# Query and key weights loaded by whole pages, their 32-column runs picked by the readers, and rows sorted by head at the store

## The chip, the cores and the metric

The kernel runs on one core of a Trainium2 chip. A core has a matrix engine (TensorE, PE in the profile, with its weight loads listed as PEld), a vector engine (VectorE, DVE), an engine for functions of one element (ScalarE, ACT), a general one (GpSimd, POOL) and a queue engine that mainly issues transfers (SyncE, SP). Each engine takes its instructions in a fixed order, and an instruction that waits holds all that stand behind it. Transfers run on 16 DMA engines; SP's are issued one after another, in the order in which the program was written. Matrix products are accumulated in PSUM banks, from which ACT or DVE moves them on.

The metric is the device time of one execution, in microseconds (us), as the median of several runs.

## The reference

The kernel computes one layer of an encoder block over 1024 tokens of width 1024, in float32. One input projection feeds two branches. Branch A is a windowed attention with three groups of eight heads of 64 dimensions, whose windows step by 1, 4 and 16 tokens. Branch B is a gated recurrence. Both are gated, projected, merged and added to the input.

What the change touches is the making of queries and keys in branch A:

```python
h = rms_norm(h_res, norm_w[layer])
z = jnp.einsum('bsd,dc->bsc', h, w_in[layer])
...
q = rms_norm(qkv_a[:, :, g, 0], q_norm_w[layer, g])   # over the 64 dimensions of a head
k = rms_norm(qkv_a[:, :, g, 1], k_norm_w[layer, g])
o_g, m_g, d_g = dilated_window_attention(q, k, v, bias, window, dilation)
```

## The kernel before, in words

**Stages.** The kernel goes through the input norm and the value projections (to about 141 us of the span), a stage of block products (to about 686), attention mixed with other products (to about 860), the recurrence (to about 1250) and the output projections.

**Block products.** A block is a product of 1024 x 256 weights with all tokens. Its weights are cut into quarters: two halves of the contraction (first digit) by two column halves of 128 (second digit), "11", "12", "21", "22", each a page of 128 partitions x 512 floats. Seven products are made instead of eight, of sums and differences of quarters: "11", "T1", "T2", "21", "T3", "22", "T4" (`run_quads`). Each of the seven is 12 matmuls in three passes per four pieces, because a float32 weight is split into a high part `whi` and a low part `wlo`. ACT makes `whi`; POOL makes `wlo`, or DVE for "T2" and "T4" (`LOWS`, line 33); DVE forms the differences in place in the raw page (line 445). There are 27 blocks: 12 of queries or keys ("qk", by group, half of the heads, and query or key), and 15 of other columns.

**Pages and rings.** Raw quarters lie in a ring `qraw` of `QRAW` = 6 buffers of 128 x 512 (line 1112); split pages lie in rings `whi` and `wlo` of `RING` = 9 buffers, which all stages share (lines 25, 349). A page is split only when its number is below the count of freed pages plus `RING` (lines 369, 437). The normalisation of queries and keys has a ring `ny` of four buffers (line 1117); the other rings are `spare` and `stage`.

**The columns of a qk block.** A page of the stored weights holds 256 query columns and then 256 key columns, four heads of 64 each. `block_pages` (line 680) takes for column half 0 the first 32 dimensions of each of the four heads and for half 1 the last 32. So a quarter is four transfers of 64 KB, one per head, in runs of 32 floats (line 413). Thus the two halves of a head lie in the same rows of two tiles, and the sum of squares over a head is one product with a 0/1 matrix (`head_sums`). The chain of each half of the tokens is: squares on ACT, their sum on DVE, split, `head_sums` on PE, logarithm and exponential on ACT (`guess`), a Newton step on DVE, the scaled result on DVE (`scaled`, line 1208), and the store to the scratch tensor `qkD` by SP. For the second and third group, `scaled` also sorts the tokens by their residue mod 4 or 16, and the store writes runs of 128 or 32 floats.

**Attention.** `load_heads` (line 1300) loads queries and keys of four heads as four transfers of 32 partitions each, which puts the dimensions of a head back together; `load_k` and `load_q` call it. The scores of the third group are 64 x 64 products with 64 neighbouring keys of a residue (line 1396).

**Order.** The program orders its own work: a planner (`Plan`) keeps an expected time per engine, with 0.08 us of SP's time for a transfer's issue (line 170), and knows which part of a buffer is written or read when (`_boxes`, which takes a view apart into pieces if its outer dimension is at most 8). A task is emitted when the planner expects its inputs and its buffer soon (`tick`; `Ring.soon`). The order on each engine is fixed by that.

Of the kernel before, what the change touches and what calls it, by code (L numbers as in the profile page):

```python
# [23 lines left out]
WARM = 10  # L24
RING = 9
RAWS = 4
# [3 lines left out]
QB = 6  # L30
QRAW, SPARE = 6, 7
RES = (1, 4, 16)
# [36 lines left out]
def _boxes(ap):  # L69

    if ap.space != SB or ap.ap[0][0] <= 0:
        return ALL
    step, n = ap.ap[0]
    p, lo = divmod(ap.offset, step)
    dims = list(ap.ap[1:])
    starts = [lo]
    while len(dims) > 1 and dims[0][1] <= 8:
        st, m = dims[0]
        if abs(st) <= sum(abs(x) * (k - 1) for x, k in dims[1:]):
            break  # L80
# [147 lines left out]
class Builder:  # L228
# [147 lines left out]
    def split(self, raw, low=None, page=None):  # L376
        hi, lo = self.hir.get(), self.lor.get()
        if self.low == "dma" and page is not None:
            self.p.act.activation(hi, raw, AF.Copy)
            self.p.act.activation(lo, hi.bitcast(F32), AF.Copy, scale=-1.0)  # L380
            self.task("pool", [lo], lambda: self.p.pool.dma_start(lo, page, accum_op=OP.add), 1)
        else:
            self.p.act.activation(hi, raw, AF.Copy)
            getattr(self.p, low or self.low).tensor_tensor(lo, raw, hi.bitcast(F32), op=OP.subtract)
        self.w[self.split_next] = (hi, lo)
        self.split_next += 1
# [18 lines left out]
    def start_quads(self, ring):  # L405

        raw = {}

        def load(m, b):
            raw[m, b] = ring.get()  # L410
            src = self.quads[m][("11", "21", "12", "22").index(b)]
            if isinstance(src, list):
                for i, x in enumerate(src):
                    self.p.sp.dma_start(raw[m, b].rearrange("p (d a c) -> p a d c", d=4, a=4)[:, i], x)
                return
            dst = raw[m, b] if len(src.shape) == 2 else raw[m, b].rearrange("p (d c) -> p d c", d=src.shape[1])
            self.p.sp.dma_start(dst, src)

        for m in range(len(self.quads)):
            for b in ("11", "12", "22", "21"):  # L420
                self.task("sp", [], lambda m=m, b=b: load(m, b), 2, ring.soon)
        work = []
# [10 lines left out]
        at = [0]  # L433
# [7 lines left out]
        def go(k):  # L441
# [6 lines left out]
            for x in {"T3": ("12",), "T4": ("11", "21"), "22": ("22",)}.get(dst, ()):  # L448
                ring.done(raw.pop((m, x)))

# [178 lines left out]
def hybrid_block(ctx, tc, a, out):  # L629
# [50 lines left out]
    def block_pages(kind, *at):  # L680
# [6 lines left out]
        if kind == "gb":  # L687
# [3 lines left out]
        p = 24 * g + 8 + 8 * hv  # L691
        return tuple([_dram(wi, (p + 4 * k) * 65536 + 256 * e + 32 * col + 64 * i, [[512, 128], [65536, 4], [1, 32]])
                      for i in range(4)]
                     for col in range(2) for k in range(2))

# [318 lines left out]
    b.low = "dma"  # L1014
    b.split_next_page()
    at = {0: {11: lambda: root(1)}, 3: {5: lambda: root_out(1), 11: lambda: root(0)}, 7: {5: lambda: root_out(0)}}
    for d in range(8):
        u_products(1, d, at.get(d, {}))
        b.free_to(d + 1)
        if d < 8 - EA:  # L1020
            square(0, EA + d, xs[0, EA + d])()
        if d < 4:
            split_u(1, 4 + d)
        if d < 7:
            b.split_next_page()
        if 3 < d < 7:
            prep_h(1, d - 4, rs["B", 1])
        b.tick()
# [74 lines left out]
    def blocks_start():  # L1103
# [7 lines left out]
        p.tile([128, 16], F32, name="blkPad")  # L1111
        blk["raw"] = b.ring(p, "qraw", QRAW, [128, 512])
        blk["spare"] = b.ring(p, "spare", SPARE, [128, 512])
# [94 lines left out]
    def scaled(g, hv, e, half, z, y2, o, col, count):  # L1208
# [10 lines left out]
        def out():  # L1219
            s_.dma_start(qkD[g, hv, 2 * e + col].rearrange("p (r u) -> p r u", r=R)[:, :, n * half:n * half + n],  # L1220
                         o.rearrange("p (r u) -> p r u", r=R))
            blk["y"].done(o)
# [76 lines left out]

    def load_heads(t, g, hv, k):  # L1300
        for j in range(2):
            for c in range(2):
                s_.dma_start(t[64 * j + 32 * c:64 * j + 32 * c + 32],
                             qkD[g, hv, k + c].rearrange("(a i d) t -> i d a t", a=2, i=2)[j])

    def load_k(g, hv):
        KT[g, hv] = att["k"].get()
        load_heads(KT[g, hv], g, hv, 2)
        score_tasks(g, hv)

    def load_q(g, hv):
        QT[g, hv] = att["q"].get()
        load_heads(QT[g, hv], g, hv, 0)
        score_tasks(g, hv)
# [60 lines left out]
    def scores(g, hv, i0):  # L1375
# [16 lines left out]
        for u in range(2):  # L1392
            k0, n = geo[u][:2]
            for p, e, j in ((p, e, j) for p in range(2) for e in range(2) for j in range(2) if g == 2):
                at = slice(k0 + 64 * e, k0 + 64 * e + 64)
                t_.matmul(pss[u][j][64 * e:64 * e + 64, p, :], q[64 * j:64 * j + 64, p, at], kT[64 * j:64 * j + 64, p, at],
                          start=True, stop=True)
# [1140 lines left out]
```

## Time and profile before

| what | value |
|---|---|
| median of three runs | 1457.58 us (1456.97 to 1460.9) |
| the profiled execution | 1453.19 us |
| its span, from first to last instruction | 1451.4 us |
| PE busy | 1426.0 us, 98% of the span |
| DVE, ACT, POOL busy | 918.3, 859.0, 330.8 us |
| DMA packets | 301347, of which 174963 under 512 B |
| granted PE clock, mean | 0.995 |

The page of the profile gives shares over the whole span. The stretches of the span (busy time of each engine between two points of time, with the count of its instructions), the chain of waits (the work that ended last, followed back) and the timeline of an engine show where time is lost. In the rows, L59 is a helper through which all instructions are issued, so rows are told apart by the names of their tiles: `qA`, `qE`, `qC` are the banks of the block products, `gp` those of the other products, `sc` the scores, `nss` the sums over a head.

### The profile page before, as it was taken

Reading aid. Unit: us, or ns where it says so; the run is one execution under the profiler, and the core shown is the slowest. Engines: PE = TensorE matmul, PEld = TensorE weight load, DVE = VectorE, ACT = ScalarE, POOL = GpSimd, SP = SyncE. Lnnn points to the kernel's source line nnn. Section 1 sums busy time; section 2 is a strip of 40 time slices with the busy share of each in tenths; the row PEclk is TensorE's granted clock in tenths of the full one; section 3 lists DMA queues with packets and bytes.
Section 4 is the critical chain, followed back from the end, with each engine's and each line's share of the span. In section 5 each row is a group of like instructions: output and inputs, shape, how many; then the busy total and the mean of one; then the engine's idle time right before and its main releaser. Section 6 shows DMA issues by size and latency. Waiting matters only on the chain.

```text
span 1451.4 us, 23558 instructions
## 1 busy us (share of the span) xinstructions
PE 1426.0 (98%) x8106; PEld 1182.5 (81%) x8106; DVE 918.3 (63%) x1859; ACT 859.0 (59%) x1852; POOL 330.8 (23%) x356
## 2 busy tenths in 40 slices
PE   9999999998999989999899999999999999999998
PEld 8788787887888868888678878888888888888887
DVE  6673466575666665631355646787878787358973
ACT  7743565554554655644478852397777774548461
POOL 0102335463333323334021000022222221001011
PEclk9999999999999999999999999999999999999999
DMA  7747678987454534533999529864444453678665
GB/s 238 181 143 173 181 205 191 183 179 142 114 117 116 104 74 114 146 102 116 236 255 244 137 76 223 231 169 107 127 108 127 107 135 91 197 257 215 185 171 137
DMA packets 301347, 230.54 MB, mean 159 GB/s; under 512 B 174963, under 2 KB 225419, under 8 KB 300716
## 3 DMA queue, kind: packets, MB, share of 16 engines
q1 hardware_dynamic: 286540, 203.69, 50.4%
q0 software_dynamic: 13824, 25.17, 11.2%
q8 instruction: 64, 1.05, 0.3%
q14 instruction: 55, 0.45, 0.1%
q10 hardware_dynamic: 864, 0.19, 0.1%
HBM read 169.04 MB, written 81.43 MB: 173 GB/s over the span
## 4 chain that ended last, share of the span: by engine, by line
PE 83%; DVE 6%; DMA 4%; ACT 4%; SPq 2%; issue 1%; POOL 0%; DVEq 0%; ACTq 0%
PE gp L59 24%; PE qA L59 19%; PE qE L59 9%; PE sA L59 6%; PE qC L59 5%; PE sE L59 5%; PE u L59 3%; PE oB L59 3%; PE o L59 2%; PE pT L59 2%; PE sc L59 2%; SPq L59 2%; DVE Bc L59 1%; PE U L59 1%; DVE S L59 1%
## 5 line engine op out<-in xcount | busy, mean ns | idle before, releaser
L59 POOL TENSOR_TENSOR wlo<-qraw,whi 128x512 fp32r<-128x512 f32 x135 | 182.3, 1352 | 396.4 <-ACT whi L59 378.5
L59 ACT ACTIVATE whi<-qraw 128x512 fp32r<-128x512 f32 x189 | 118.1, 627 | 116.7 <-PE qA L59 32.6
L59 DVE TENSOR_TENSOR qraw<-qraw,qraw 128x512 f32<-128x512 f32 x108 | 94.1, 872 | 39.4 <-DMA qraw<-in_w_in_dram 32.3
L59 PE MATMUL gp<-hh,whi 128*128 128x512 f32 x264 | 109.7, 415 | 0.0
L59 PE MATMUL gp<-hh,wlo 128*128 128x512 f32 x264 | 103.6, 393 | 0.0
L59 PE MATMUL gp<-hl,whi 128*128 128x512 f32 x264 | 103.0, 390 | 0.0
L59 ACT ACTIVATE as<-as,neg 128x192 f32<-128x192 f32 (+2 forms) x192 | 80.3, 424 | 21.6 <-DVE neg L59 21.5
L59 ACT ACTIVATE whi<-raw 128x512 fp32r<-128x512 f32 x92 | 57.2, 627 | 47.1 <-DMA raw<-in_w_in_dram 21.0
L59 PE MATMUL qA<-hh,whi 128*128 128x512 f32 x216 | 84.0, 389 | 0.0
L59 PE MATMUL qA<-hl,whi 128*128 128x512 f32 x216 | 84.0, 389 | 0.0
L59 PE MATMUL qA<-hh,wlo 128*128 128x512 f32 x216 | 84.0, 389 | 0.0
L59 PE MATMUL gp<-whi,hh 128*128 128x512 f32 x192 | 78.8, 411 | 0.0
L59 POOL COPY mm<-Bc 128x8 f32<-128x8 f32 x64 | 32.6, 539 | 197.7 <-DVE Bc L59 123.3
L59 PE MATMUL gp<-wlo,hh 128*128 128x512 f32 x192 | 75.4, 393 | 0.4 <-DVE wlo L59 0.4
L59 PE MATMUL gp<-whi,hl 128*128 128x512 f32 x192 | 75.2, 392 | 0.0
L59 DVE CUSTOM_DVE_ANT_0 as<-sc,abias 128x192 f32<-128x192 f32 (+2 forms) x192 | 52.0, 326 | 36.3 <-PE sc L59 27.5
L59 DVE TENSOR_TENSOR wlo<-qraw,whi 128x512 fp32r<-128x512 f32 x54 | 37.4, 692 | 56.8 <-ACT whi L59 56.7
L59 DVE TENSOR_TENSOR ny<-ny,spare 128x512 f32<-128x512 f32 x48 | 65.9, 1392 | 0.4
L59 ACT ACTIVATE spare<-qA 128x512 f32<-128x512 f32 x51 | 30.2, 592 | 58.7 <-PE qA L59 57.7
L59 PEld LDWEIGHTS gp<-hh,wlo 128*128 128x128 f32 x264 | 49.5, 188 | 11.0
L59 POOL DMA_DIRECT2D wlo<-in_w_in_dram x36 | 31.3, 870 | 113.8 <-ACT wlo L59 98.0
L59 PEld LDWEIGHTS gp<-hh,whi 128*128 128x128 f32 x264 | 49.8, 189 | 8.3
(309 smaller groups left out, 4118.3 us busy)
## 6 DMA issues: line engine op xcount, KB each, us to landing
raw<-in_w_in_dram SPq DMA_DIRECT2D x84, 256.0 KB, 3.7
qraw<-in_w_in_dram SPq DMA_DIRECT2D x60, 256.0 KB, 3.4
qraw<-in_w_in_dram SPq DMA_DIRECT2D x192, 64.0 KB, 2.7
qkD<-ny SPq DMA_DIRECT2D x48, 256.0 KB, 3.4
wlo<-in_w_in_dram POOLq DMA_DIRECT2D x36, 256.0 KB, 4.3
sg<-sgD SPq DMA_DIRECT2D x32, 256.0 KB, 3.6
eraw<-wsD SPq DMA_DIRECT2D x32, 256.0 KB, 3.4
sgD<-stage SPq DMA_DIRECT2D x26, 256.0 KB, 2.1
```

Of the source, the lines that this page charges most:

```text
L59: got = f(*args, **kw)
```

## The change

Loads: the two column halves of a half of the contraction share one buffer of 128 x 1024 (four such buffers instead of six of 128 x 512). For a qk block one transfer of 512 KB loads both, in runs of 256 floats, and the two quarters are views of it with 16 runs of 32 floats. Other blocks load each quarter into its half of the buffer, as before. A buffer is free when both quarters are done with. Stores: each normalised tile is written by four transfers of 32 rows, to where the head's dimensions lie together in `qkD`. For the keys of the third group, a store no longer puts the two halves of the tokens between each other; the scores pick the keys in two runs of 32. Attention loads queries and keys with one transfer of 1 MB each. The `whi` and `wlo` rings have 8 buffers instead of 9, so one page fewer is split ahead, and in the first stage a split that stood before a loop now is the last of it. `_boxes` takes apart views with up to 16 pieces.

```diff
-RING = 9
+RING = 8
...
-QRAW, SPARE = 6, 7
+QRAW, SPARE = 4, 7
...
-    while len(dims) > 1 and dims[0][1] <= 8:
+    while len(dims) > 1 and dims[0][1] <= 16:
...
     def split(self, raw, low=None, page=None):
-        hi, lo = self.hir.get(), self.lor.get()
+        tiles = hi, lo = self.hir.get(), self.lor.get()
+        if len(raw.shape) == 3:
+            hi, lo = (t.rearrange("p (x i) -> p x i", i=raw.shape[2]) for t in tiles)
...
-        raw = {}
+        raw, pair, left = {}, {}, {}
 
         def load(m, b):
-            raw[m, b] = ring.get()
-            src = self.quads[m][("11", "21", "12", "22").index(b)]
-            if isinstance(src, list):
-                for i, x in enumerate(src):
-                    self.p.sp.dma_start(raw[m, b].rearrange("p (d a c) -> p a d c", d=4, a=4)[:, i], x)
+            half, col = int(b[0]) - 1, int(b[1]) - 1
+            if (m, half) not in pair:
+                pair[m, half] = ring.get()
+                left[m, half] = 2
+            t = pair[m, half]
+            pages = self.quads[m]
+            if len(pages) == 2:
+                for c in range(2):
+                    raw[m, f"{half + 1}{c + 1}"] = t.rearrange("p (x c i) -> p c x i", c=2, i=32)[:, c]
+                self.p.sp.dma_start(t.rearrange("p (d c) -> p d c", d=4), pages[half])
                 return
+            raw[m, b] = t[:, 512 * col:512 * col + 512]
+            src = pages[("11", "21", "12", "22").index(b)]
...
+        def drop(m, b):
+            half = int(b[0]) - 1
+            raw.pop((m, b))
+            left[m, half] -= 1
+            if left[m, half] == 0:
+                ring.done(pair[m, half])
+
         for m in range(len(self.quads)):
-            for b in ("11", "12", "22", "21"):
-                self.task("sp", [], lambda m=m, b=b: load(m, b), 2, ring.soon)
+            for b in ("11", "22") if len(self.quads[m]) == 2 else ("11", "12", "22", "21"):
+                self.task("sp", [], lambda m=m, b=b: load(m, b), 2,
+                          lambda m=m, b=b: (m, int(b[0]) - 1) in pair or ring.soon())
...
-        return tuple([_dram(wi, (p + 4 * k) * 65536 + 256 * e + 32 * col + 64 * i, [[512, 128], [65536, 4], [1, 32]])
-                      for i in range(4)]
-                     for col in range(2) for k in range(2))
+        return tuple(_dram(wi, (p + 4 * k) * 65536 + 256 * e, [[512, 128], [65536, 4], [1, 256]]) for k in range(2))
...
     b.low = "dma"
-    b.split_next_page()
...
-        if d < 7:
-            b.split_next_page()
+        b.split_next_page()
...
-        blk["raw"] = b.ring(p, "qraw", QRAW, [128, 512])
+        blk["raw"] = b.ring(p, "qraw", QRAW, [128, 1024])
...
         def out():
-            s_.dma_start(qkD[g, hv, 2 * e + col].rearrange("p (r u) -> p r u", r=R)[:, :, n * half:n * half + n],
-                         o.rearrange("p (r u) -> p r u", r=R))
+            for i in range(4):
+                to = qkD[g, hv].rearrange("a p t -> (a p) t")[256 * e + 64 * i + 32 * col:256 * e + 64 * i + 32 * col + 32]
+                x = o[32 * i:32 * i + 32]
+                if g == 2 and e == 1:
+                    s_.dma_start(to[:, 512 * half:512 * half + 512], x)
+                else:
+                    s_.dma_start(to.rearrange("p (r u) -> p r u", r=R)[:, :, n * half:n * half + n],
+                                 x.rearrange("p (r u) -> p r u", r=R))
             blk["y"].done(o)
...
-    def load_heads(t, g, hv, k):
-        for j in range(2):
-            for c in range(2):
-                s_.dma_start(t[64 * j + 32 * c:64 * j + 32 * c + 32],
-                             qkD[g, hv, k + c].rearrange("(a i d) t -> i d a t", a=2, i=2)[j])
-
...
-        load_heads(KT[g, hv], g, hv, 2)
+        s_.dma_start(KT[g, hv], qkD[g, hv, 2:4].rearrange("a p t -> p a t"))
...
-        load_heads(QT[g, hv], g, hv, 0)
+        s_.dma_start(QT[g, hv], qkD[g, hv, 0:2].rearrange("a p t -> p a t"))
...
-                t_.matmul(pss[u][j][64 * e:64 * e + 64, p, :], q[64 * j:64 * j + 64, p, at], kT[64 * j:64 * j + 64, p, at],
+                keys = kT[64 * j:64 * j + 64, p].rearrange("k (h r n) -> k r h n", h=2, r=16)[:, k0 // 64 + e]
+                t_.matmul(pss[u][j][64 * e:64 * e + 64, p, :], q[64 * j:64 * j + 64, p, at], keys,
```

More of the change, by code (lines that the diff above doesn't have):

```diff
@@ L384, in split @@
             getattr(self.p, low or self.low).tensor_tensor(lo, raw, hi.bitcast(F32), op=OP.subtract)
-        self.w[self.split_next] = (hi, lo)
+        self.w[self.split_next] = tiles
         self.split_next += 1
@@ L448, in go @@
             for x in {"T3": ("12",), "T4": ("11", "21"), "22": ("22",)}.get(dst, ()):
-                ring.done(raw.pop((m, x)))
+                drop(m, x)
         for k, (eng, *_) in enumerate(work):
```

## The prediction

> **What bounds the kernel now.** I read the page's busy table first, then stretches of the span, then the chain of waits with the timelines of TensorE (PE), ScalarE (ACT) and the SP queue at the stretches in which PE falls short.
>
> ```profile
> span 1451.4 us, 23558 instructions
> PE 1426.0 (98%) x8106; PEld 1182.5 (81%) x8106; DVE 918.3 (63%) x1859; ACT 859.0 (59%) x1852; POOL 330.8 (23%) x356
> ...
> 186.12 2.72 PE qE L59 x12
> ```
>
> PE is at work nearly all the time, and inside the block stage its pace is even: twelve matmuls in 2.72 us, 0.2267 us each. Consecutive matmuls overlap in the records, so a stretch is judged by its count times 0.2267. In steady stretches that fills the stretch. It does not in these (stretch, then PE busy and count; the last three columns are granted clock, DMA share, GB/s):
>
> ```profile
> 153.50:155.10 1.60, 0.15 (x2) 0.11 (x1) 1.60 (x3) 1.27 (x3) 0.57 (x1) 1.00 1.15 411
> 230.50:236.00 5.50, 4.32 (x18) 2.85 (x17) 2.17 (x3) 5.44 (x10) 4.73 (x6) 1.00 0.32 34
> 310.00:345.00 35.00, 30.13 (x127) 24.27 (x126) 19.61 (x23) 18.51 (x32) 17.22 (x17) 0.95 0.70 139
> 345.00:523.00 178.00, 178.00 (x785) 146.98 (x784) 118.26 (x140) 98.75 (x171) 60.83 (x46) 1.00 0.50 112
> 523.00:546.00 23.00, 18.72 (x69) 14.08 (x68) 12.33 (x16) 13.78 (x25) 5.22 (x4) 0.85 0.40 83
> 702.00:712.00 10.00, 6.13 (x79) 4.90 (x78) 3.05 (x36) 3.16 (x17) 0.00 (x0) 0.83 0.95 241
> 721.50:726.00 4.50, 2.16 (x67) 1.80 (x67) 1.74 (x9) 2.52 (x15) 0.00 (x0) 1.00 1.08 322
> ```
>
> 345 to 523 is the yardstick: 785 x 0.2267 = 178.0, nothing lost. The losses are A (near 155) 1.45 us; D (230) 5.5 - 18 x 0.2267 = 1.4; B (near 335) 35 - 28.8 = 6.2; C (near 535) 23 - 15.6 = 7.4; at the start of attention E1 3.9 us idle plus a lower clock (0.83 of 10 us is at most 1.7), taken as 4.9, and E2 4.5 - 2.2 = 2.3. Together 23.7 us. Only these can be won; everything else the change saves is covered by a PE that has no gap.
>
> What stands behind them:
>
> ```profile
> 122.10 14.65 SPq L59 DMA_DIRECT2D qraw<-in_w_in_dram  x24
> ...
> 155.00 0.50 PE L59 MATMUL qA<-S2h,whi 128*128 128x512 f32 x1 [1.45 <-ACT spare L59]
> ...
> 323.73 1.57 DVE L59 TENSOR_TENSOR ny<-ny,spare 128x512 f32<-128x512 f32 x1
> ...
> 318.98 11.66 SPq L59 DMA_DIRECT2D qraw<-in_w_in_dram  x10
> 330.74 1.21 SPq L59 DMA_DIRECT2D qkD<-ny  x2
> ...
> 336.52 1.15 ACT L59 ACTIVATE ny<-spare 128x512 f32<-128x512 f32 x2 [6.43 <-issue]
> ...
> 338.20 0.80 PE L59 MATMUL qA<-S2h,whi 128*128 128x512 f32 x1 [4.87 <-ACT stage L59]
> ...
> 526.43 5.91 DMA qkD<-ny
> ...
> 704.49 0.29 PE L59 MATMUL sc<-ak,aq 64*64 64x64 f32 x2 [1.98 <-issue]
> 706.67 0.60 PE L59 MATMUL sc<-ak,aq 64*64 64x64 f32 x12 [1.89 <-DMA av<-vD]
> ...
> PE sc L59 <- DMA abias<-skewD: 1.1, 1, 1.1
> ```
>
> B, step by step: DVE finishes a normalised half at 325.3 (323.73 + 1.57). Its store is issued only at 330.74, because a train of ten weight-piece loads fills SP's queue until then. The `ny` buffer comes free when the store has landed, ACT waits 6.43 us for it with an evacuation of PE's bank queued behind, and PE stands 4.87 us; the rest of B's 6.2 is the clock that was granted afterwards (0.95 over the stretch). (PE's row names that evacuation; the pass over `ny` ahead of it is what waited.) C is a store again, this one 5.91 us from issue to landing, after DVE's products; only a short train (four loads) stands ahead of it. A is the same queue: 24 loads take 14.65 us at the stage's start, and what is loaded behind them comes late. E1 waits for the last pieces of queries and keys (the name `av` in the row belongs to a load issued after them), E2 for the bias behind the next such pieces.
>
> **The change, part by part.**
>
> ```profile
> qraw<-in_w_in_dram SPq DMA_DIRECT2D x192, 64.0 KB, 2.7
> qkD<-ny SPq DMA_DIRECT2D x48, 256.0 KB, 3.4
> ...
> ak<-qkD SPq DMA_DIRECT2D x24, 256.0 KB, 6.3
> aq<-qkD SPq DMA_DIRECT2D x24, 256.0 KB, 8.7
> ...
> L59 SPq DMA_DIRECT2D qraw<-in_w_in_dram x252: 327/505/3127, 122.1 to 645.0; - x126
> L59 SPq DMA_DIRECT2D qkD<-ny x48: 319/524/717, 184.1 to 604.7; - x48
> ```
>
> *Loads of query and key weights.* 192 issues become 24 (12 blocks x 2), each of 512 KB in 1 KB runs instead of 128 B runs. SP saves 168 x 0.505 = 85 us of issuing; the trains behind A and B, 24 and 10 long, become 4 and 2. Off the path otherwise.
>
> *Stores.* 48 issues become 192, each of 32 rows. That is 144 x about 0.5 (the row of 64 KB loads) = 72 us more of SP. So per block SP's work barely falls (20 issues to 18), but it is put elsewhere: a half's two columns now need 8 issues, 4.0 us, where they needed 2 x 0.52 = 1.05. The last piece goes out about 3 us later if SP is otherwise idle, and about 5 us earlier than before where a train stood ahead (B). Next to wait is the same ACT pass over `ny`. A quarter of the stores (keys of the third group) also become 2 KB runs; cost nothing, gain nothing on PE.
>
> The Trainium skill (DMA: Bandwidth & Descriptors, "Anatomy of one DMA" and "Measured") speaks against this split: about 2.0 us fixed per DMA, and 64 KB as the size below which the fixed part rules. Were the pieces served one after another, a store would land 6 us later, which would be rival 2. The rows above say the fixed parts overlap: 64 KB pieces are issued 0.5 us apart and land in 2.7 us against 3.4 for 256 KB, so 1.5 us later per column is what I use.
>
> *Loads of queries and keys for attention.* 48 issues become 12. Stretches at their first use, same columns:
>
> ```profile
> 700.00:702.00 2.00, 2.00 (x11) 1.65 (x10) 0.00 (x0) 0.17 (x1) 0.00 (x0) 1.00 1.08 225
> 702.00:704.00 2.00, 0.51 (x3) 0.09 (x1) 0.00 (x0) 0.00 (x0) 0.00 (x0) 1.00 1.03 217
> 706.00:708.00 2.00, 1.33 (x49) 1.36 (x53) 0.07 (x1) 0.00 (x0) 0.00 (x0) 0.63 1.09 318
> ```
>
> The DMA engines are full throughout, but move 217 to 225 GB/s while the 32-partition pieces of `ak` and `aq` flow and 318 otherwise. 2.1 MB at 220 is 9.5 us, at 318 it is 6.6: 2.9 us sooner, and six issues fewer (about 6 x 0.5) stand before the bias load that E2 waits for. I take 3.3 of E1's 4.9 and 1.2 of E2's 2.3: 4.5, with 0 and 7.2 as ends.
>
> The Trainium skill (SBUF — State Buffer, "Door 1: The DMA port swizzle") gives a reason: 32 or 64 neighbouring partitions reach 8 of the 16 ports. These rows agree. By that rule the new 32-row stores run at the lower rate too, 1.2 us instead of 0.8 for 256 KB; that is inside the store's lateness above.
>
> *Readers with 32-column runs.* ACT, DVE and POOL now read [16 x 32] with gaps.
>
> ```profile
> L59 DVE TENSOR_TENSOR qr<-qr,q 128x512 f32<-128x512 f32 x32 | 21.9, 685 | 0.0
> L59 ACT ACTIVATE km<-q,lomlb 128x256 f32<-128x256 f32 x32 | 15.8, 495 | 0.0
> L59 ACT ACTIVATE km<-qr,lomlb 128x256 f32<-128x256 f32 x32 | 15.8, 495 | 0.0
> L59 DVE TENSOR_TENSOR q<-q,q 128x256 f32<-128x256 f32 x32 | 13.4, 418 | 0.0
> L59 POOL TENSOR_TENSOR wlo<-qraw,whi 128x512 fp32r<-128x512 f32 x135 | 182.3, 1352 | 396.4 <-ACT whi L59 378.5
> ```
>
> `q<-q,q` reads 64-element runs with gaps: half the elements of `qr<-qr,q` in 418 of 685 ns, no gap penalty. ACT reads gapped `qr` and plain `q` in the same 495. For POOL no row has gaps; bounds 1352 ns and, by DVE's strided product above (1.57 against 0.685, 2.3 times), 3.1 us: 60 x 1.75 = 105 us more, still inside 396 us of idle. Taken: nothing. The gapped key operand of the third group's scores: taken as nothing, too.
>
> *Weight ring 9 to 8.* One page less is split ahead, outside the blocks too. Two places are tight:
>
> ```profile
> 50.15 0.63 ACT L59 ACTIVATE whi<-raw 128x512 fp32r<-128x512 f32 x1 [0.81 <-PE u L59]
> 51.74 0.86 POOL L59 DMA_DIRECT2D wlo<-in_w_in_dram  x1 [1.85 <-ACT wlo L59]
> ...
> wlo<-in_w_in_dram POOLq DMA_DIRECT2D x36, 256.0 KB, 4.3
> ...
> 58.55 0.39 PE L59 MATMUL gp<-wlo,hh 128*128 128x512 f32 x1
> 102.99 0.50 PE L59 MATMUL gp<-wlo,hh 128*128 128x512 f32 x1 [0.35 <-DVE wlo L59]
> ```
>
> The eighth page of the second set is split at 50.15; its accumulating load goes out at 51.74 and takes 4.3 (median). It is first used in the unit that ends at 58.55. Split one weight page later (12 x 0.2267 = 2.7 us, and a small product that stands between, about 0.9), at 53.8, it lands at 53.8 + 1.6 + 4.3 = 59.7: 1.2 us lost. At 103 the last page is already 0.35 late; its buffer comes free six matmuls, 1.36 us, later: 1.3 lost. Sum 2.5, ends 0 and 5.
>
> **The sum.** Won: A 1.45, B 6.2, C half of 7.4 (its store is held less by loads than by DVE's strided products and its own landing, and those stay), D 0, E 4.5: 15.9. Lost: ring 2.5; new stalls where the later last piece holds ACT, taken as 4 (ends 0 and 18, priced below). Net -9.4. The profiled execution took 1453.19 us, 1.8 outside its span: 1443.8. The runs' median is 1457.58, 4.4 above it, so in those terms 1448.2.
>
> **Rivals.**
> 1. *The queue work only moves* (no change). For it: 20 issues to 18 per block. Then B and C are traded for stalls like them, and A, E and the ring leave -1.45 - 4.5 + 2.5 = -3.5, or +3 with one more stall of B's size: 1454 to 1460, about 1457. Against: the store in B stood 5.4 us behind loads, not behind stores.
> 2. *Slower: the four-piece store holds ACT.* The place is the pass over `ny` (squares, then inverse roots) of the next half, in 24 halves. The kernel's planner reckons 0.08 us per issue where 0.5 is paid, so it orders that pass about 3 us too soon. It decides once ACT is held longer than about 2.7 us, one operation of twelve matmuls; B shows what 6.43 us cost. Six such halves at 3 us each with the slower clock after them: +18; less A and E, plus the ring: +14, 1472. At four halves, +8: 1466.
> 3. *All goes:* every loss above but D is cured and the ring costs nothing: -22.3, 1435. C speaks against it.
> 4. *The loads are not what it says* (a store still queued behind whole pages waiting for a buffer): two loads wait as ten did. It ends as rival 1 and is counted there.
>
> **Chances.** Forecast 0.47; rival 3 0.13; rival 1 with 4 0.25; rival 2 0.15. A difference below 0.3% (4.4 us) can't be told from none here, so faster 0.60, same 0.25, slower 0.15. The range 1437 to 1461 holds forecast and rival 1, and leaves out rival 2 and the far end of 3; the forecast's own range is 1443 to 1453.
>
> **What would show it.** Right: loads of `qraw` for these blocks as 24 issues with no train above 4; PE in step near 155 and 335; `ak` and `aq` landing with the DMA rate above 300 GB/s and the first scores by about 703. Right on the ring: PE waiting on `wlo` near 59 and more than 0.35 us near 103. Wrong: ACT waiting on `qkD<-ny` in more than four places, `wlo<-qraw` on POOL far above 1352 ns with PE waiting for it, or the block stage (155 to 686) no shorter.

## The result, and the profile after

The change takes 1448.94 us (1446.71 to 1453.23, six runs) against 1457.55 us: 0.9945 of the time before, 95% interval 0.9926 to 0.9964. Timed again beside the experiments it took 1451.66 us against 1457.8: 0.9958 (0.9946 to 0.997). So 6.1 to 8.6 us are won, somewhat less than the 9.4 forecast, and much of it is not won where the forecast put it.

From the page of the changed kernel:

```profile
span 1451.5 us, 23314 instructions
PE 1425.5 (98%) x8106; PEld 1179.9 (81%) x8106; DVE 912.9 (63%) x1860; ACT 858.4 (59%) x1852; POOL 330.1 (23%) x355
...
L59 POOL TENSOR_TENSOR wlo<-qraw,whi 128x512 fp32r<-128x512 f32 x135 | 183.0, 1358 | 397.9 <-ACT whi L59 390.0
...
qraw<-in_w_in_dram SPq DMA_DIRECT2D x24, 512.0 KB, 5.1
qkD<-ny SPq DMA_DIRECT2D x192, 64.0 KB, 2.1
```

The span is that of the profile before (1451.4). The equality misleads, because single executions of one kernel differ by some us. PE runs the same 8,106 matmuls in every kernel here (their order differs in parts of the block stage, in `issue05` in later stages too), so the time between the starts of, say, the 451st and the 671st can be compared stage by stage. This table is worked out from the traces in that way (us; matmuls counted from the first; two stages that differ by at most 1.5 us are left out; the last column is the ratio of the timed runs):

| kernel | to the 451st | 451st to 671st | blocks, 671st to 2401st | attention, 3010th to 4001st | merge, 4001st to 5101st | ratio |
|---|---|---|---|---|---|---|
| before | 103.3 | 51.7 | 409.1 | 84.9 | 149.9 | 1 |
| before, again | 102.9 | 51.6 | 410.7 | 87.4 | 151.2 | - |
| after | 106.2 | 50.0 | 406.1 | 80.6 | 154.1 | 0.9945 |
| after, again | 107.9 | 50.0 | 406.1 | 81.2 | 151.5 | 0.9958 |
| ring8 | 106.0 | 50.0 | 410.5 | 84.6 | 151.2 | 1.0021 |
| loads | 106.8 | 50.0 | 405.3 | 87.4 | 151.2 | 0.9984 |
| stores | 103.7 | 51.1 | 422.8 | 79.9 | 154.5 | 1.0002 |
| smallloads | 107.4 | 50.0 | 406.4 | 79.6 | 152.5 | 0.9959 |
| ring9 | 102.8 | 50.0 | 419.3 | 77.9 | 152.3 | 1.0010 |
| ring9loads | 103.8 | 50.0 | 420.6 | 86.4 | 151.4 | 1.0042 |
| ring9s | 102.9 | 50.1 | 440.0 | 80.6 | 151.9 | 1.0151 |
| hyb | 102.9 | 50.0 | 412.5 | 80.3 | 151.7 | 0.9982 |
| issue05 | 107.5 | 49.9 | 411.6 | 83.1 | 150.5 | 0.9989 |
| bstore | 102.9 | 50.5 | 404.8 | 86.3 | 154.9 | 0.9953 |

The first profile of before was a lucky execution, in its attention above all (its second took 1459.47 us); the first profile of after was an unlucky one in the merge (154.1, the second time 151.5). Apart from the merge the change shows: about 4 us lost at the start, 1.7 won to the 671st matmul, 3 to 4.6 won in the blocks, 4 to 7 in attention. The two profiles of each kernel are only 3.1 us apart on average (spans 1451.4 and 1457.7 before, 1451.5 and 1451.4 after), so the stages add up to less than the 6.1 to 8.6 us of the timed runs.

The stretches of the changed kernel (columns as in the prediction):

```profile
230.00:240.00 10.00, 8.27 (x29) 6.06 (x28) 6.72 (x11) 6.85 (x13) 4.80 (x6) 0.83 0.91 179
310.00:345.00 35.00, 33.42 (x145) 26.76 (x144) 24.63 (x28) 20.82 (x37) 18.55 (x18) 1.00 0.82 167
345.00:523.00 178.00, 174.85 (x765) 143.00 (x764) 110.58 (x133) 97.95 (x172) 61.09 (x46) 1.00 0.42 114
523.00:546.00 23.00, 21.73 (x95) 17.43 (x94) 18.29 (x22) 15.21 (x28) 9.16 (x6) 1.00 0.30 78
...
692.00:696.00 4.00, 4.00 (x19) 3.30 (x19) 1.38 (x2) 1.27 (x2) 0.00 (x0) 1.00 0.91 293
696.00:700.00 4.00, 4.00 (x20) 3.30 (x19) 0.01 (x1) 1.88 (x2) 0.00 (x0) 1.00 1.00 374
```

By count times 0.2267: B lost 6.2 and loses 2.1 now (35 - 145 x 0.2267); C lost 7.4 and loses 1.5; but D, over these ten us, loses 3.4 instead of 1.6, and the yardstick 345 to 523, which lost nothing, loses 4.6. The bytes for attention now flow at 293 and 374 GB/s (before, in the same two stretches, at 228 and 226). What PE waits for, from PE's timeline:

```profile
55.60 0.50 PE L59 MATMUL gp<-whi,hh 128*128 128x512 f32 x1 [1.96 <-ACT stage L59]
...
105.19 0.50 PE L59 MATMUL gp<-wlo,hh 128*128 128x512 f32 x1 [1.03 <-DVE wlo L59]
...
233.41 0.50 PE L59 MATMUL nss<-nlo,headones 128*128 128x512 f32 x1 [0.84 <-DVE nlo L59]
...
235.15 0.79 PE L59 MATMUL nss<-nlo,headones 128*128 128x512 f32 x1 [0.88 <-DVE nlo L59]
...
320.05 0.50 PE L59 MATMUL qA<-S2h,whi 128*128 128x512 f32 x1 [1.16 <-ACT spare L59]
```

The last of these comes back with each later block, at 400.49 and 480.91. And ScalarE's timeline at two of them:

```profile
53.68 0.63 ACT L59 ACTIVATE whi<-raw 128x512 fp32r<-128x512 f32 x1 [1.70 <-PE u L59]
54.34 0.63 ACT L59 ACTIVATE wlo<-whi 128x512 fp32r<-128x512 f32 x1
54.88 1.83 ACT L59 ACTIVATE stage<-u,rr 128x512 f32<-128x512 f32 x3
...
316.98 0.63 ACT L59 ACTIVATE nhi<-ny 128x512 fp32r<-128x512 f32 x1 [2.27 <-DVE ny L59]
...
319.42 0.58 ACT L59 ACTIVATE spare<-qA 128x512 f32<-128x512 f32 x1
```

At 55 a page is split as soon as PE frees its ring slot, and PE's own evacuation (`stage<-u`) stands behind the split. At 320 an evacuation stands behind `nhi<-ny`, which waits 2.27 us for DVE. In neither row is a DMA what is waited for.

### The profile page after: what moved, and what is told of

Its sections match the earlier page's. It is cut to its first block, busy times and chain, and to the rows that moved or that the text cites. A ratio compares the mean times of both kernels' runs of the same rounds, so it can differ in the third digit from the quotient of the medians.

```text
span 1451.5 us, 23314 instructions
## 1 busy us (share of the span) xinstructions
PE 1425.5 (98%) x8106; PEld 1179.9 (81%) x8106; DVE 912.9 (63%) x1860; ACT 858.4 (59%) x1852; POOL 330.1 (23%) x355
## 3 DMA queue, kind: packets, MB, share of 16 engines
q0 software_dynamic: 13824, 25.17, 11.3%
## 5 line engine op out<-in xcount | busy, mean ns | idle before, releaser
L59 POOL TENSOR_TENSOR wlo<-qraw,whi 128x512 fp32r<-128x512 f32 x135 | 183.0, 1358 | 397.9 <-ACT whi L59 390.0
L59 DVE TENSOR_TENSOR qraw<-qraw,qraw 128x512 f32<-128x512 f32 x81 | 71.1, 878 | 65.0 <-POOL wlo L59 65.0
L59 PE MATMUL gp<-hh,wlo 128*128 128x512 f32 x264 | 103.7, 393 | 0.0
L59 ACT ACTIVATE as<-as,neg 128x192 f32<-128x192 f32 (+2 forms) x192 | 80.3, 424 | 17.2 <-DVE neg L59 17.1
L59 DVE TENSOR_TENSOR ny<-ny,spare 128x512 f32<-128x512 f32 x48 | 59.2, 1257 | 0.4
```

The costliest lines, as they stand in the source:

```text
L59: got = f(*args, **kw)
```

## The experiments

**One part of the change at a time.** `ring8` is the kernel before with the ring of 8 and the moved page splits; `loads` is the change without its stores and attention loads; `stores` is the kernel before with only these two.

```diff
# ring8: on the kernel before
-RING = 9
+RING = 8
...
-    b.split_next_page()
...
-        if d < 7:
-            b.split_next_page()
+        b.split_next_page()
# loads: on the changed kernel, stores and attention loads back
-            for i in range(4):
...
+            s_.dma_start(qkD[g, hv, 2 * e + col].rearrange("p (r u) -> p r u", r=R)[:, :, n * half:n * half + n],
+                         o.rearrange("p (r u) -> p r u", r=R))
...
-        s_.dma_start(KT[g, hv], qkD[g, hv, 2:4].rearrange("a p t -> p a t"))
+        load_heads(KT[g, hv], g, hv, 2)
# stores: the same lines of the kernel before, the other way round
```

Expected of the changed kernel, run again with them:

> The changed kernel once more, for a second profile and a closer interval. Two readings of the first profile, whose 1453.23 us is no shorter than the 1453.19 of the profile before: (a) that execution had a stall of chance, 4.2 us in the merge of the attention outputs near 930 (PE waits for `al` behind DVE's `og`), which another execution lacks; then the second profile takes 1447 to 1450 and TensorE's lag there is under 1 us, while the losses near 55, 104, 232, 319, 399 and 479 come back to within 0.5 us, since they follow from the written order. (b) The stall near 930 belongs to the change; then it is there again. Ratio expected 0.993 to 0.996 by the timed runs so far.

Of `ring8`:

> The kernel before with the weight ring cut from 9 to 8 and the page splits moved as in the change, nothing else. My prediction's sum: 2.5 us slower (1.2 near 59, 1.3 near 103), about 1460. By the trace of the changed kernel: 2.1 near 54 and 1.3 near 104, 3.4 us slower, 1461, if nothing later takes the lag back. Rival: the later stalls near 155 and 232 take the lag back, since what they wait for does not depend on TensorE; then within 1 us of before.

Of `loads`:

> The change with its loads of the weight pages and its ring of 8, but the stores of normalised rows and the attention loads as before. By my prediction: A 1.45, B 6.2 and half of C 3.7 won, ring 2.5 to 3.4 lost: 8 to 9 us faster, 1449, with no stall of 2 us at 319, 399 and 479, if those come from the four-piece stores (theory S). If they come from the order in which DVE, ACT and POOL now split the weight quadrants (theory L, to which the trace of the changed kernel inclines: ACT waits there for a DVE sum that ran beside a POOL split, not for a store), they are here too, 5 to 6 us, and the gain is 2 to 4 us, 1454. Attention starts as late as before in both.

Of `stores`:

> The kernel before with the four-piece stores sorted by head and the single attention loads alone (small weight loads, ring of 9). By my prediction: E1 and E2 give 4.5 us, A stays, B stays or grows by up to 3 us (the store's last piece goes out 3 us later behind the same train of ten loads), C stays: 1 to 5 us faster, 1453 to 1457. Theory S adds the stalls near 319, 399 and 479, 5 to 6 us: 0 to 2 us slower. Rival 2 of the prediction (the four-piece store holds ACT by itself) gives 8 to 14 us slower.

Measured: `after_again` 1451.66 us in the median, but its profiled execution took 1453.13, not the 1447 to 1450 of reading (a). PE loses 1.6 us in the merge there instead of 4.2, of which the second profile of before, further down, shows 1.2 as well. So most of that loss was chance, as (a) had it. `ring8` takes 1459.93 us (ratio 1.0009 to 1.0032), `loads` 1455.8 (0.9974 to 0.9994), `stores` 1458.48 (0.9989 to 1.0015). By their ratios `loads` and `stores` give -2.3 and +0.3 us, the whole change -6.1, so the parts do not add.

Rows of `ring8`, from the timelines of PE, DVE and SP:

```profile
55.36 0.50 PE L59 MATMUL gp<-whi,hh 128*128 128x512 f32 x1 [1.96 <-ACT stage L59]
...
104.92 0.50 PE L59 MATMUL gp<-wlo,hh 128*128 128x512 f32 x1 [1.03 <-DVE wlo L59]
...
124.61 14.00 SPq L59 DMA_DIRECT2D qraw<-in_w_in_dram  x24
...
155.90 0.39 PE L59 MATMUL qA<-S2h,whi 128*128 128x512 f32 x1
...
296.01 0.69 DVE L59 TENSOR_TENSOR qraw<-qraw,qraw 128x512 f32<-128x512 f32 x1 [5.13 <-DMA qraw<-in_w_in_dram]
...
299.77 0.80 PE L59 MATMUL qA<-S2h,whi 128*128 128x512 f32 x1 [2.38 <-ACT spare L59]
...
323.69 0.50 PE L59 MATMUL qA<-S2h,whi 128*128 128x512 f32 x1 [1.16 <-ACT spare L59]
```

Both waits before 106 and the stall near 320 (here 323.69) belong to the ring of 8, with old loads and old stores. So theories S and L both fall. `ring8` comes out at the 1460 of the prediction's sum for the ring, but not in that way: it loses 3 us at the start, wins A, B and most of C, and has the new stalls. It has no gap A, although the train of 24 loads stands there at full length (14.00 us), and PE is in step at 155.90. Nor has it B, though a train of ten stands there as well, and C is down to 2 us. Its PE stalls once more, at 299.77, behind weights for which DVE waited 5.13 us.

One reason shows in the order in which the programs' instructions stand. Call moved the fewest operations that must be taken out for the rest to stand in the same order. Of ScalarE's 510 operations from the 671st matmul to the 3010th, 163 are moved between before and `ring8`, and 169 between before and the change. Between the change and `ring8` 29 are moved, between the change and `loads` none, on any engine, and between before and `stores` nine. So the planner writes one order for a ring of 9 and another for a ring of 8. At B the difference can be read from ScalarE's timelines, first of before, then of after:

```profile
337.57 0.58 ACT L59 ACTIVATE stage<-qA 128x512 f32<-128x512 f32 x1
```

```profile
336.73 0.60 ACT L59 ACTIVATE stage<-qA 128x512 f32<-128x512 f32 x1 [1.56 <-PE qA L59]
...
337.74 1.14 ACT L59 ACTIVATE ny<-spare 128x512 f32<-128x512 f32 x2
```

Before, the evacuation for which PE stood (`stage<-qA`) came behind the pass over `ny` that waited for the store (336.52, shown in the prediction). In the changed kernel it comes ahead of that pass. `ring8` has it ahead as well (340.34, the pass at 341.36). At A it is alike: before, the evacuation `spare<-qA` at 154.36 stands behind two splits of late weights; in `ring8`, at 153.38, ahead of them. No run changes the order alone, so how much of the other stalls is due to it is read from such rows, not shown.

Since `loads` keeps the change's order in the blocks to the last operation, the two tell what the four-piece stores cost in that order: 406.1 - 405.3 = 0.8 us. What the single attention loads win is 87.4 - 80.9 = 6.5 us in these profiles; the eight profiles with single loads have 80.4 on average in that column, the six of before, `before_again`, `ring8`, `loads`, `ring9loads` and `bstore` 86.2, which makes 5.8. Nearly all of it falls in the first 290 matmuls, where the averages are 19.1 and 24.3 and no profile of one kind reaches the other. The timed runs put single loads and four-piece stores together at 4 us (1455.8 against 1451.66).

In `stores`, whose order is near that of before, ScalarE waits for a store six times, 11.3 us in all, against about 9 before (B among them). PE stands 3.18 us at B (347.39 there) and, new, 2.23 at 508.65 behind two of these waits. So there the pieces do hold ScalarE now and then, but 11 of the 13.7 us that `stores` loses in the blocks arise near 208 and 237, where ScalarE waits 0.5 us at most for a store.

**A second profile of before, the ring back at 9, and the planner's price of an issue.**

```diff
# ring9: on the changed kernel (page splits as before)
-RING = 8
+RING = 9
-QRAW, SPARE = 4, 7
+QRAW, SPARE = 3, 7
# ring9s: the same with
+QRAW, SPARE = 4, 5
# issue05: on the changed kernel
-            self.t[key] = start + (1.0 if key == "pool" else 0.08)
+            self.t[key] = start + (1.0 if key == "pool" else 0.5)
```

> The kernel before once more, for a second profile. Its first profile (1453.19 us) is 4.4 us below the runs' median; all four other profiles so far lose 1.2 to 2.6 us against it in the merge near 930 and 0.8 near 1252, places that the edits do not touch. If that first profile was lucky there, this one shows the same two losses (2 to 4 us) and takes 1455 to 1459, with B near 335 and C near 530 as before. If the losses are not there, they belong to the edits.

> The changed kernel with the weight ring back at 9 and the page splits where they were, the room taken from the pair ring (4 to 3 buffers). Theory R (from the ring-alone kernel, which shows them with the old loads and stores): the waits near 54 and 104 and the stalls near 232, 319, 399 and 479 all come from the ring of 8. Then they go, 3.4 + 2.3 + 3 x 2.2 = 12 us; but the order of the ring of 8 also showed no stall C near 530, so up to 7 of these come back. Expected 1441 to 1448. Rival: the stalls come from the weights' halves being split in pairs, or three pair buffers starve the splits; then only the 3.4 us near 54 and 104 are won, 1448, or it is no faster than the change, 1452.

> The same with the ring of 9 and four pair buffers, the room taken from the evacuation buffers (`spare` 7 to 5). Theory R expects what it expects of the version with three pair buffers, 1441 to 1448, if five evacuation buffers are enough; if they are not, ScalarE's evacuations wait for stores of `spare` and the block stage gets longer, 1455 or more.

> The changed kernel with the planner's cost of a DMA issue on SP at 0.5 us, as the traces show, in place of 0.08. My prediction held that the planner orders the pass over `ny` too soon because of that error and that ScalarE is then held for stores. If so, ScalarE's waits on the store go and 1 to 4 us are won, 1448 to 1451. Rival: ScalarE is held by stores nowhere that TensorE feels it, and the new order makes no difference or has stalls of its own: 1450 to 1456.

Measured: `before_again` 1459.47 us: against the first profile 1.2 us more near 930, 0.5 near 1252 and, not expected, 1.6 in the blocks, nearly all of it at B, and 2.5 in attention, where no edit was made either; A and C as before.

`ring9` 1459.63 us (0.9992 to 1.0027): the ring's loss at the start is gone (102.8 in the table), but the blocks take 419.3. Theory R was right about the stalls that it named and wrong about the time. The yardstick stretch of `ring9` loses nothing again:

```profile
345.00:523.00 178.00, 178.00 (x785) 146.95 (x784) 112.65 (x137) 102.00 (x178) 63.69 (x48) 1.00 0.42 115
```

What took their place are stalls near 208, 240, 327 and 545. ScalarE's order is nearly that of before (11 operations moved, on DVE 80), but the raw ring has three buffers, room for six quarters, and DVE waits for weights eight times for more than 1.5 us, ahead of 208 (at 205.59) and of 327 (at 319.13) among others. With whole loads and a ring of 9, `ring9` has no gap A, and no wait for a store at B.

`ring9s` 1480.38 us (1.0133 to 1.0168): with five evacuation buffers the blocks take 440.0. The expected cause, evacuations that wait for stores of `spare`, is not in its trace; PE waits for ScalarE's `nhi`, 24.2 us in all. `issue05` 1454.27 us (0.9972 to 1.0007): telling the planner the true price gives another order, with 411.6 in the blocks, and nothing won.

**Order held, queue work changed.** For `smallloads` the changed kernel loads each block's weights by 16 transfers again, while the planner is told of the whole load: PE, DVE, ACT and POOL keep their order to the last operation. `ring9loads` is `ring9` with one-piece stores and the old attention loads, which in the blocks has the order of `ring9`. `hyb` has the ring of 9 but lets the blocks' splits run only 8 pages ahead.

```diff
# smallloads: on the changed kernel
-                self.p.sp.dma_start(t.rearrange("p (d c) -> p d c", d=4), pages[half])
+                whole = t.rearrange("p (d c) -> p d c", d=4)
+                quarter = t.rearrange("p (d a c i) -> p d a c i", d=4, a=4, c=2)
+                for c in ((0, 1), (1, 0))[half]:
+                    for i in range(4):
+                        self.p.sp.real.dma_start(quarter[:, :, i, c], pages[half][:, :, 64 * i + 32 * c:64 * i + 32 * c + 32])
+                self.p.note("sp", "dma_start", (whole, pages[half]), {})
# hyb: on ring9
-            if at[0] != k or (n is not None and (self.split_next != n or n >= self.freed + self.RING)):
+            if at[0] != k or (n is not None and (self.split_next != n or n >= self.freed + self.RING - 1)):
```

> The changed kernel with the weights of the query and key blocks loaded by 16 DMAs of 64 KB per block again, into the same paired buffers; the planner is told of one whole load, so that PE, DVE, ACT and POOL keep the order of the changed kernel to the last operation. What it loses is the queue work of the loads alone. My prediction's sum: A 1.45, B 6.2 and half of C 3.7 come back, 11 us, 1463. By the stage table of the runs (155 to 564: ring-alone kernel 410.5, which has nearly this order and small loads, against 405.3 with whole loads): 4 to 5 us, 1456, with weight data late for DVE behind trains of ten loads near 295. Rival: in this order nothing waits for the loads, within 1 us of the change, 1452.

> The version with ring 9 and three pair buffers, but one-piece stores and the attention loads of before; its order on PE, DVE, ACT and POOL in the blocks is that of the ring-9 version with four-piece stores, operation for operation. If the stalls of that version near 208, 240, 325 and 545 (10 us) come from the four-piece stores in the order of ring 9, they go: blocks 404 to 410 us instead of 419, attention 5 to 6 longer: 1449 to 1455. If three pair buffers or the order itself make them, the blocks stay at 415 or more and the whole is 1460 or more.

> The changed kernel with a weight ring of 9 and three pair buffers, but splits of the blocks' weights held to 8 pages ahead, as in the change. Theory: the ring of 8 costs 3 to 4 us before 104, and it is its order in the blocks that is good (406 us against 419 with ring 9 and the same stores). This version has the first without the cost and about a tenth of ScalarE's operations in the blocks moved against the second: 1446 to 1449. Rival: a tenth moved is enough for stalls of its own, 1450 to 1460.

`smallloads` takes 1451.59 us, ratio 0.9959 (0.9943 to 0.9974), against 0.9958 with whole loads. The rival was right in the time: with this order and this room the loads' queue work is worth nothing. Its timelines of SP and ACT where B was, and a stretch:

```profile
331.17 11.79 SPq L425 DMA_DIRECT2D qraw<-in_w_in_dram  x16
343.06 2.73 SPq L59 DMA_DIRECT2D qkD<-ny  x4
...
338.57 0.60 ACT L59 ACTIVATE stage<-qA 128x512 f32<-128x512 f32 x1 [1.56 <-PE qA L59]
...
339.59 1.14 ACT L59 ACTIVATE ny<-spare 128x512 f32<-128x512 f32 x2
...
349.34 0.63 ACT L59 ACTIVATE ny<-spare 128x512 f32<-128x512 f32 x1 [5.00 <-DMA qkD<-ny]
```

```profile
310.00:345.00 35.00, 33.41 (x145) 26.74 (x145) 23.97 (x27) 19.63 (x35) 17.90 (x17) 1.00 0.81 144
```

A train of 16 loads again takes 11.79 us, and a four-piece store is issued behind it at 343.06 (332.37 with whole loads). ScalarE's pass over `ny` then waits 5.00 us for that store, nearly as long as at B before (6.43). Yet PE does the same 145 matmuls in the stretch and has no gap of 0.4 us from there to 402, because the evacuation that it needs has already been made, at 338.57. So the late store and ScalarE's wait are there again; what is missing is an evacuation behind them for which PE would have to stand.

`ring9loads` takes 1463.79 us (1.0028 to 1.0057), blocks 420.6: the stalls of `ring9` are still there with one-piece stores, so the four-piece stores don't make them. At the first of them, SP and DVE in `ring9loads`:

```profile
199.99 1.41 SPq L59 DMA_DIRECT2D qraw<-in_w_in_dram  x3
...
205.94 0.69 DVE L59 TENSOR_TENSOR qraw<-qraw,qraw 128x512 f32<-128x512 f32 x1 [2.46 <-DMA qraw<-in_w_in_dram]
```

and in `stores`:

```profile
202.16 5.40 SPq L59 DMA_DIRECT2D qraw<-in_w_in_dram  x10
...
207.04 0.69 DVE L59 TENSOR_TENSOR qraw<-qraw,qraw 128x512 f32<-128x512 f32 x1 [2.42 <-DMA qraw<-in_w_in_dram]
```

DVE waits 2.4 us for weights in both, with three whole loads or with ten small ones. ScalarE's split of these weights stands ahead of `nhi<-ny` there, so PE's head sums wait as well; before, `nhi` stood ahead of the split, and DVE waited 1.38 us at that place (205.39). So the form of the loads does not decide it. Nine to eleven operations of ScalarE stand elsewhere than before, but so do some of DVE and POOL, and which of them matter was not tried. (The profiled executions of `stores` and `ring9loads` were the longest of their runs, so their block columns are upper ends.)

`hyb` takes 1454.17 us (0.9971 to 0.9993): the start is cured (102.9), and the blocks lose 6 us against the change. It has the 1.16 us stalls near 320, 402 and 483, which `ring9` has not, so these go with splitting 8 pages ahead, not with the number of buffers. Its largest other losses are two stalls, from the timelines of DVE and PE:

```profile
227.71 0.69 DVE L59 TENSOR_TENSOR qraw<-qraw,qraw 128x512 f32<-128x512 f32 x1 [4.09 <-DMA qraw<-in_w_in_dram]
...
231.65 0.50 PE L59 MATMUL nss<-nlo,headones 128*128 128x512 f32 x1 [2.93 <-DVE nlo L59]
...
377.82 0.69 DVE L59 TENSOR_TENSOR qraw<-qraw,qraw 128x512 f32<-128x512 f32 x1 [6.70 <-DMA qraw<-in_w_in_dram]
...
380.23 0.50 PE L59 MATMUL qA<-S2h,whi 128*128 128x512 f32 x1 [1.75 <-ACT spare L59]
```

Both follow weights that came late. 58 of ScalarE's operations are moved against the change, but the rows point at the raw ring, which has room for six quarters here and for eight in the change.

**Was B read rightly?** The last run takes the kernel before and issues two of its 48 stores from POOL's queue, in the order as it was.

```diff
         def out():
-            s_.dma_start(qkD[g, hv, 2 * e + col].rearrange("p (r u) -> p r u", r=R)[:, :, n * half:n * half + n],
-                         o.rearrange("p (r u) -> p r u", r=R))
+            to = qkD[g, hv, 2 * e + col].rearrange("p (r u) -> p r u", r=R)[:, :, n * half:n * half + n]
+            x = o.rearrange("p (r u) -> p r u", r=R)
+            k = blk["stored"] = blk.get("stored", -1) + 1
+            (g_ if k in (18, 19) else s_).real.dma_start(to, x)
+            b.p.note("sp", "dma_start", (to, x), {})
```

> The kernel before with the two stores of the half at B (those issued at 330.74 in its first profile, behind the train of ten loads) put on POOL's queue, and nothing else; PE, ACT and DVE keep their order to the last operation. If B is what my prediction says (the store stands behind the train, the buffer comes free late, ACT waits), the two stores go out near 323.5 and 325.5 and have landed by 330, ACT's wait of 6.43 us near 336 shrinks to under 1.5, TensorE's gap of 4.87 us near 338 goes, and the time falls by 5 to 6 us, 1452. Rival: the gap is made by the weights, which are late behind the same train, or by the order of ACT's and DVE's work; then the gap stays at 3 us or more and the time at 1457.

Measured: 1451.86 us, ratio 0.9953 (0.9937 to 0.997). Its timelines of SP, POOL, ACT and PE:

```profile
317.38 12.70 SPq L59 DMA_DIRECT2D qraw<-in_w_in_dram  x10
...
321.88 0.82 POOL L1223 DMA_DIRECT2D qkD<-ny  x1 [3.21 <-DVE ny L59]
...
325.28 0.77 POOL L1223 DMA_DIRECT2D qkD<-ny  x1 [1.26 <-DVE ny L59]
...
330.38 0.63 ACT L59 ACTIVATE ny<-spare 128x512 f32<-128x512 f32 x1 [0.42 <-DMA qkD<-ny]
...
331.55 0.50 PE L59 MATMUL qA<-S2h,whi 128*128 128x512 f32 x1
```

The train of ten still takes 12.70 us. The stores no longer stand behind it, ACT waits 0.42 us instead of 6.43, and PE has no gap at all at the place where it stood 4.87 us. Stretch 310 to 345 in `before_again`, then in `bstore`:

```profile
310.00:345.00 35.00, 29.52 (x121) 23.75 (x120) 18.65 (x23) 18.42 (x32) 16.30 (x16) 0.90 0.69 132
```

```profile
310.00:345.00 35.00, 35.00 (x155) 28.54 (x154) 25.71 (x30) 19.61 (x35) 19.48 (x19) 1.00 0.89 168
```

Two stores on another queue win as much as the whole change (0.9953 against 0.9945 and 0.9958). The two together were not tried.

## Why the prediction was right, and where its steps failed

The number was right: 1448.2 forecast, 1448.94 and 1451.66 measured. Of the sum behind it A, E and the ring came out in about their size. In the blocks the terms B, C, D and new stalls were forecast at -5.9 together and measured at -3.6, and not for the reasons that the forecast gave. That the total still fits is in part luck.

| term | forecast | measured | what the runs showed |
|---|---|---|---|
| A | -1.45 | -1.7 | gone with whole loads (`ring9`), but also with the ring of 8 and the train of 24 |
| B | -6.2 | -4.1 (6.2 to 2.1) | diagnosis right, cure another |
| C | -3.7 | -5.9 (7.4 to 1.5) | mostly won by `ring8` alone (2.1 left) |
| D | 0 | +1.8 (1.6 to 3.4) | in `ring8` too |
| new stalls | +4 | +4.6 (345 to 523) | in `ring8` too; from splitting 8 pages ahead, not from the stores |
| E | -4.5 | about -5 | the single loads, as argued |
| ring | +2.5 | +3.9 at the start | second place right, first by another way |

*The step that failed* is "Loads of query and key weights": that the trains behind A and B become 4 and 2 long, and that this is what wins A and B. The trains did become short (four at 124.88, where 24 stood). But with the trains put back and the order kept, the time is the same (0.9959 against 0.9958). In nearly the old order whole loads do remove gap A and the wait at B (`ring9`), but other stalls of the same size come there. What removed the stalls in the changed kernel is what the edit did elsewhere. The ring of 8 made the planner write another order, with about a third of ScalarE's operations in the blocks moved, and the raw ring got room for eight quarters instead of six. The prediction spoke of the planner only for one term; it took the old order as given in all others, and it gave the room of the raw ring no term at all.

*B's diagnosis* (store behind the train, buffer late, ACT held, PE held) was right in every link, as `bstore` shows. A right diagnosis was taken for proof that the change's remedy would be the one at work. What matters is whether an evacuation that PE needs stands behind the wait; the new order put it ahead, and then the train was harmless.

*Rival 2* and the term for stalls by the four-piece stores: the pieces went out at 0.548 us each (median) and landed after 2.1 us instead of 3.4. ACT's passes over `ny` waited on `qkD<-ny` nowhere in the changed kernel's profiles; one split, at 380.98 in the first, waited 2.09 us. In this order the stores cost 0.8 us, not 4. In `stores` a stall of rival 2's kind is there, 2.23 us long. The Trainium skill (DMA: Bandwidth & Descriptors, "Anatomy of one DMA") gives each DMA on GpSimd's path a fixed part of about 2 us. These rows, from SP's queue, agree with a fixed part but show that the parts overlap, as the prediction took it. The planner's price of 0.08 us, on which rival 2 leaned, was an error without a gain in it: `issue05` wins nothing by mending it.

*The ring.* Near 104 the wait came as worked out (forecast 1.3; the lag, by which a matmul starts later than before, grows by 1.3). Near 54 the forecast had 1.2 us for a page that lands late. The lag grows by 2.3 us there, in the second profile by 3.9, and PE waits for its evacuation, which stands behind the later split on ACT (the rows at 53.68 to 54.88). `ring8` as a whole is 2.1 us slower by the medians, close to the 2.5, but it holds gains and losses in the blocks that the term does not speak of.

*E* was argued from the rate while `ak` and `aq` flow (217 to 225 GB/s), and the rate rose to 293 and 374. The first scores start at 703.28 and 704.86 in the two profiles; the wait ahead of them is not shorter (2.47 and 2.35 us, before 1.98), but the second wait, of 1.89, is gone.

*Readers with runs of 32* cost nothing, as taken: POOL's split 1358 ns against 1352, ScalarE's 627 in both.

*Rival 1* (queue work only moves) was right that in the order of the change shorter trains win nothing by themselves, but B and C were not traded for stalls of their size: the blocks became 3 to 4.6 us shorter, and the time fell below its 1454 to 1460.

What stays open is how the gain in the blocks divides between the order and the room of the raw ring. With room for six quarters (before twice, `ring8`, `stores`, `ring9`, `ring9loads`, `hyb`, `bstore`) DVE waits four to ten times for weights for more than 1.5 us between 140 and 700; with eight (the change twice, `loads`, `smallloads`, `issue05`, `ring9s`) never or once. So the 4 us between `ring8` (410.5) and the changed kernel (406.1) look like the room, and the stall of `ring8` at 299.77 behind a wait of 5.13 us bears that out. But 29 operations of ScalarE stand elsewhere as well, and no run changes the room alone.

## What to carry to other kernels

Where a planner writes the order, an edit to a transfer or a ring also changes the order, and a few operations that stand elsewhere can be worth more than the edit. Tell the two apart by holding the order (tell the planner of one transfer, issue the other) before a gain is credited to the edit. Look also for what the edit changed beside the transfer, such as the room of a ring. A long train of loads was harmless here unless a store stood behind it, a pass waited for that store, and behind the pass stood an evacuation that PE needed; then two stores on an idle queue won as much as the whole change.

## What was not expected of the hardware

The same stall costs different amounts in two executions of the same program. Stretch 53 to 59 of the changed kernel, first profile and second:

```profile
53.00:59.00 6.00, 4.04 (x18) 3.01 (x17) 1.51 (x4) 5.29 (x10) 1.31 (x3) 1.00 0.88 187
```

```profile
53.00:59.00 6.00, 4.04 (x13) 2.84 (x12) 1.51 (x4) 5.24 (x10) 1.31 (x3) 0.76 0.89 200
```

The wait itself is the same (1.96 us, PE busy 4.04 in both), but the second execution does 13 matmuls instead of 18, at a granted clock of 0.76. The Trainium skill (TensorE: Matmul & The Clock Gate, "Part 1: The HAM clock gate (the "warmup" mystery)") says that the clock follows how busy PE was in windows of about 3.4 us that run freely; that would give such a lottery, and these rows agree with it. They do not agree that a whole window must be idle, as that section has it: 1.96 us were enough in one of the two. This may make part of the few us by which runs of one kernel differ here. By these two executions a stall of 2 us costs 2.3 (10 matmuls fewer than before) to 3.4 (15 fewer).

A DVE operation that takes 0.69 us elsewhere took 1.78 while a split on POOL, itself 1.60 instead of 1.30, ran beside it; its end is what ACT waits for at 316.98. That the one slowed the other is read from the rows; no run was made on it. Timelines of POOL and DVE, first profile of after:

```profile
314.79 1.60 POOL L59 TENSOR_TENSOR wlo<-qraw,whi 128x512 fp32r<-128x512 f32 x1 [2.69 <-ACT whi L59]
...
315.16 1.78 DVE L59 TENSOR_TENSOR ny<-ny,ny 128x512 f32<-128x512 f32 x1
```
